# An encoder layer on one core: the transposes of an even chunk's linear attention output and their copy, set earlier in the second sweep

## The chip, the core and the metric

The kernel runs on one core of a Trainium2 chip. A core has a matrix engine (TensorE, PE in the profile, with its weight loads as PEld), a vector engine (VectorE, DVE), a scalar engine for activations and copies (ScalarE, ACT), a general one (GpSimd, POOL), and SyncE (SP), which here issues nearly all DMAs. Each engine works through its own instructions in their order and waits on semaphores for what it needs from others. The metric is the device time of one execution in microseconds (us), lower is better.

## What is computed

One layer of a hybrid encoder on a sequence of 2048 rows of width 1024, in float32. An input projection feeds two groups. Group A is a bidirectional gated linear attention with 4 heads, worked in chunks; group B is a latent attention with 4 heads, whose queries and keys come from compressed and normalised projections, with a rotary part. Both outputs go through one output projection, a residual and a layer norm.

```
h = x @ w_in
g_q, g_k, g_v, g_gate, g_lr_f, g_lr_b, m_cq, m_ckv, m_kr, m_gate = split(h)
o_a = rms_norm(gla(fwd) + gla(bwd)) * silu(g_gate)          # group A
o_b = softmax(q_nope k_nope' + q_rope k_rope') v * silu(m_gate)   # group B
out = layer_norm(alpha * x + concat(o_a, o_b) @ w_out)
```

What matters here is the piece of group A at the end: the sum of both directions is normalised per head, multiplied by the gate, and turned so that the features lie on the partitions, as the output projection needs it.

## The kernel before

Products are made in a split form: an operand is cut into a high and a low part, and three products (high by high, high by low, low by high) are added up. Suffixes `h` and `l` on names mean these parts.

The program has a first sweep over the 16 chunks of 128 rows (backward direction, group A), a second sweep over them in the other direction (`sweep_c`, line 1219), the attention of group B, and the output projection. The change touches the second sweep alone. It runs in 8 steps, numbered 0 to 7 here, of two chunks each, an even one and an odd one. A chunk needs, among others:

- `c_ip`: the products `ipm` of the chunk's rows with the weights of the compressed queries and keys; from them ScalarE and VectorE make `cq`, `ckv` and the rotary key `krs`
- `c_tm` (line 1438): four transposes `tm` of `cq` (two), `ckv` and `krs`; copies of them are `cqT`, `ckvT` and (`c_krT`) the key's rotary part. These are the "q's and kv's parts"
- `c_pqr` and `c_tq`: the rotary queries, turned in `tq`, and read by `c_qrTh` on ScalarE and `c_qrTl` (line 1490) on VectorE
- `c_Ob`: the products `Ob` of group A with the state; `c_og` then writes `og`, the normalised and gated output
- `c_ot` (line 1576): four transposes of `og` into the PSUM tile `ot`
- `c_oT` (line 1581): the copy of `ot` to the SBUF tile `oT` on ScalarE, scaled by the norm's weight
- `c_soT` (line 1585): the store of `oT` to DRAM, issued by SP
- `c_xh`, `c_xl`: the high part `xch` of the next rows on ScalarE and their low part `xcl` on GpSimd

A step also has the gate of group B for both chunks: the products `pz` in eight pieces of twelve (`c_pz`), three passes of ScalarE over `gm` and one of VectorE (`c_gm1` to `c_gm4`), and the products `pq` of the queries with their high and low part (`c_qah`, `c_qal`) and the stores of these.

The order of all this is written out by hand. Each part has a place: a number in units of a step, counted from the start of its own step, in the table `PLACE_C` (line 169), with a pair of numbers where the even and the odd chunk have one each. Step 0 takes its numbers from `PLACE_C_FIRST`, step 7 from `PLACE_C_LAST`. All parts of all steps are sorted by step plus place and issued in that order, and `in_order` (line 416) ties each engine to it, SP too:

```
p = PLACE_C[n]
p = (last and PLACE_C_LAST.get(n)) or (not st and PLACE_C_FIRST.get(n)) or p
todo.append((st + (p if j is None else p[j]), len(todo), fn, a))
...
for _, _, fn, a in sorted(todo, key=lambda e: e[:2]):
    with self.in_order(last):
        fn(*a)
```

So a place of 1.736 lies in the next step at 0.736, beside what that step has there.

Two pools matter. The PSUM pool `tr` (line 554) has two buffers, shared by `tm`, `pqr`, `tq` and `ot` of all chunks: a new tile takes a buffer when the last reader of the one before is through. The SBUF pool `w1` (line 1223) has one buffer for each name, unless a number is given; `oT` has one:

```
self.w1 = ctx.enter_context(self.tc.tile_pool(name="wk2", bufs=1, reuse_waits="tile"))
d["oT"] = self.w1.tile([P, H, P], F32, tag="oT", name=f"oT{d['c']}")
```

Some places of steps 1 to 6, before the change (even chunk, odd chunk): `tm` 0.532 and 1.152, `ot` 0.926 and 1.312, `oT` 0.998 and 1.347, `soT` 1.119 and 1.736, `qrTl` 1.25 and 1.687, `vh` 0.732 and 1.218, `krT` 0.848 and 1.233, `pqr` 0.849 and 1.355. The next step's `xch` for its even chunk stands at 0.81 of a step, the `gm` passes at 0.823 to 0.837. The pieces of `pz` stand at 0.25 to 0.559. The store of the odd chunk in step 0 stands at 1.538.

Of the kernel before, what the change touches and what calls it, by code (L numbers as in the profile page):

```python
# [174 lines left out]
    tm=(0.532, 1.152),  # L175
    pqr=(0.849, 1.355),
    tq=(1.06, 1.482),
    ot=(0.926, 1.312),
    xh=(-0.19, -0.054),
    qhb=(-0.048, 0.321),  # L180
    MMh=(-0.034, 0.412),
# [9 lines left out]
    ckvTh=(0.64, 1.277),  # L191
    krT=(0.848, 1.233),
    qrTh=(1.16, 1.587),
    oT=(0.998, 1.347),
    oib=(0.24, 0.881),
    oia=(0.235, 0.863),
    ss=(0.278, 1.005),
# [60 lines left out]
    ot=(1.009, 1.378),  # L258
# [15 lines left out]
    oT=(1.14, 1.433),  # L274
# [49 lines left out]
    ot=(0.915, 1.082),  # L324
# [15 lines left out]
    oT=(1.011, 1.153),  # L340
# [2092 lines left out]
```

## Time and profile before

| | |
|---|---|
| median of three runs | 1276.6 us (1276.45 to 1277.14) |
| the profiled execution | 1275.83 us |
| its span, first to last instruction | 1274.0 us |
| TensorE busy | 1253.9 us, 98% of the span |
| VectorE, ScalarE, GpSimd busy | 938.3, 875.2, 849.4 us |
| second sweep | from about 378 us to some 606 us |
| one of its steps | about 30 us |

The profile is of one execution. Busy time of TensorE is from the start of a product to its modelled end, and products overlap, so that a busy engine may still have a little room. A row of the timeline has the start, the duration, the engine, the line, the operation, the tiles (out<-in, without buffer numbers), the operand shapes and the count; in brackets stand the idle time of the engine before it and what ended that. A row of the list of waits has who waited, for whom, the total in us, how often, and the longest. A row of the table of stretches has the stretch, its length, then busy time and count of PE, PEld, DVE, ACT and POOL, the granted TensorE clock, the share of the DMA engines and what they moved in GB/s. A row of the DMA issues has the tiles, the queue, the count, the size of each and the median time from issue to landing.

### The profile page before, as it was taken

To read this page: it belongs to the slowest core of one execution; us is meant where nothing else is said; L and a number is where in the kernel's file an instruction comes from. 1 tells how busy PE (TensorE), PEld (TensorE's weight loads), DVE (VectorE), ACT (ScalarE), POOL (GpSimd) and SP (SyncE) were. 2 spreads that over 40 slices of the span, in tenths; PEclk is the share of its full clock that TensorE was granted. 3 is DMA by queue.
4 is the path that set the end of the run, shared out by engine and by line. 5 is a ranking of instruction groups with operands and counts; after the bars stand their busy time and mean duration, and the time that the engine had idled before them with its cause. 6 is when DMAs were issued, how large, how long until landed. Compare 5 with 4: busy or idle time off the path is not lost.

```text
span 1274.0 us, 20184 instructions
## 1 busy us (share of the span) xinstructions
PE 1253.9 (98%) x6928; PEld 1109.6 (87%) x6928; DVE 938.3 (74%) x1702; ACT 875.2 (69%) x1553; POOL 849.4 (67%) x550
## 2 busy tenths in 40 slices
PE   7999999999999999999999999999999999999997
PEld 7999999999989999999788888888888888788886
DVE  6866675656675455555798888888888888738897
ACT  7765656766675655665688888888888888624365
POOL 0144545363667666672188888889999999965774
PEclk9999999999999999999999999999999999999999
DMA  9332524353575565565601111121223111568962
GB/s 300 96 96 63 168 81 156 106 155 102 191 254 169 180 222 184 182 196 166 177 1 42 42 42 42 42 58 59 59 58 91 53 43 31 174 207 297 342 214 98
DMA packets 122518, 166.81 MB, mean 131 GB/s; under 512 B 18502, under 2 KB 71118, under 8 KB 121776
## 3 DMA queue, kind: packets, MB, share of 16 engines
q1 hardware_dynamic: 114256, 163.39, 40.2%
q0 software_dynamic: 768, 2.10, 0.5%
q8 instruction: 55, 0.90, 0.4%
q10 hardware_dynamic: 7392, 0.03, 0.3%
q14 instruction: 47, 0.39, 0.2%
HBM read 106.72 MB, written 58.75 MB: 130 GB/s over the span
## 4 chain that ended last, share of the span: by engine, by line
PE 88%; ACT 3%; POOL 2%; DVE 2%; DMA 2%; issue 1%; SPq 1%; DVEq 0%; POOLq 0%; ACTq 0%
PE o L454 4%; PE o L456 4%; PE pS L1649 4%; PE o L455 4%; PE pS L1651 4%; PE pS L1650 4%; PE pS L1652 4%; PE pS L1653 4%; PE ipa L454 4%; PE ipa L456 4%; PE ipa L455 4%; PE pz L455 2%; PE pz L456 2%; PE pz L454 2%; PE ipg L454 2%; PE ipg L455 2%
## 5 line engine op out<-in xcount | busy, mean ns | idle before, releaser
L406 POOL TENSOR_TENSOR pl<-s,ph 128x1024 fp32r<-128x1024 f32 x128 | 306.1, 2414 | 56.4 <-ACT ph L400 56.4
L1671 DVE TENSOR_TENSOR rm<-pS,rm 128x512 f32<-128x512 f32 x210 | 144.7, 689 | 26.3 <-ACT s L1658 20.7
L1695 DVE TENSOR_TENSOR s<-s,mb 128x1024 f32<-128x1024 f32 x128 | 151.1, 1212 | 9.4 <-PE mb L1689 9.3
L1658 ACT ACTIVATE s<-pS 128x1024 f32<-128x1024 f32 x128 | 131.2, 1025 | 37.6 <-PE pS L1653 33.2
L400 ACT ACTIVATE ph<-s 128x1024 fp32r<-128x1024 f32 x128 | 134.9, 1057 | 13.4 <-PE o L456 12.7
L1699 ACT ACTIVATE s<-s 128x1024 f32<-128x1024 f32 x128 | 131.4, 1051 | 13.4 <-DVE s L1695 13.3
L454 PE MATMUL ipa<-wah,xah 128*128 128x384 f32 (+1 forms) x384 | 130.2, 339 | 6.3 <-ACT wah L400 6.2
L1112 POOL TENSOR_TENSOR Us<-Us,cw 128x512 f32<-128x512 f32 x16 | 18.2, 1134 | 175.8 <-DVE Us L1110 167.7
L455 PE MATMUL ipa<-wal,xah 128*128 128x384 f32 (+1 forms) x384 | 125.2, 326 | 0.1
L456 PE MATMUL ipa<-wah,xal 128*128 128x384 f32 (+1 forms) x384 | 125.2, 326 | 0.0
L1649 PE MATMUL pS<-qh,ckvT_h 128*128 128x512 f32 x256 | 102.5, 401 | 0.8 <-DVE rm L1671 0.4
L454 PE MATMUL o<-ph,vh 128*128 128x512 f32 x256 | 101.1, 395 | 0.0
L1652 PE MATMUL pS<-rh,krs 128*128 128x512 f32 x256 | 99.8, 390 | 0.0
L1650 PE MATMUL pS<-ql,ckvT_h 128*128 128x512 f32 x256 | 99.8, 390 | 0.0
L456 PE MATMUL o<-ph,vl 128*128 128x512 f32 x256 | 99.8, 390 | 0.0
L1651 PE MATMUL pS<-qh,ckvT_l 128*128 128x512 f32 x256 | 99.8, 390 | 0.0
L1653 PE MATMUL pS<-rl,krs 128*128 128x512 f32 x256 | 99.8, 390 | 0.0
L455 PE MATMUL o<-pl,vh 128*128 128x512 f32 x256 | 99.8, 390 | 0.0
L1722 DVE TENSOR_TENSOR ap<-ap,s 128x512 f32<-128x512 f32 x120 | 83.1, 693 | 3.5 <-ACT ap L1714 0.7
L454 PEld LDWEIGHTS ipa<-wah,xah 128*128 128x128 f32 x384 | 73.4, 191 | 7.3 <-ACT wah L400 6.7
L454 PE MATMUL pz<-xch,wzh 128*128 128x256 f32 x256 | 74.8, 292 | 0.0
L455 PEld LDWEIGHTS ipa<-wal,xah 128*128 128x128 f32 x384 | 73.4, 191 | 1.3 <-DVE wal L406 0.7
(446 smaller groups left out, 3895.9 us busy)
## 6 DMA issues: line engine op xcount, KB each, us to landing
xcf<-xT_dram SPq DMA_DIRECT2D x16, 512.0 KB, 4.9
xr<-x_dram SPq DMA_DIRECT2D x16, 512.0 KB, 6.9
xaf<-xT_dram SPq DMA_DIRECT2D x14, 512.0 KB, 3.8
wb<-wO_dram SPq DMA_DIRECT2D x16, 256.0 KB, 3.0
oib<-oi_s SPq DMA_DIRECT2D x16, 256.0 KB, 3.8
qdb<-qd_s SPq DMA_DIRECT2D x16, 256.0 KB, 4.3
SU<-su_s SPq DMA_DIRECT2D x16, 256.0 KB, 4.6
ub<-u_s SPq DMA_DIRECT2D x16, 256.0 KB, 4.2
```

The source lines that it names most:

```text
L400: return nc.scalar.activation(dst, src, AF.Copy).ins
L406: return e.tensor_tensor(dst, src, hi.bitcast(F32), ALU.subtract).ins
L454: mm(out, ah, bh, start=start, stop=False)
L455: mm(out, ah, bl, start=False, stop=False)
L456: mm(out, al, bh, start=False, stop=stop)
L1649: mm(ps[:, e], kh, qh, start=True, stop=False)
L1650: mm(ps[:, e], kh, ql, start=False, stop=False)
L1651: mm(ps[:, e], kl, qh, start=False, stop=False)
L1652: mm(ps[:, e], kr, rh, start=False, stop=False)
L1653: mm(ps[:, e], kr, rl, start=False, stop=True)
L1671: V.tensor_tensor(d["rm"], src[:, e], d["rm"], ALU.max)
L1695: V.tensor_tensor(s, s, d["mb"][:, None, :].to_broadcast([P, 2, QB]), ALU.subtract)
```

## The change

In the table for steps 1 to 6 two numbers differ, both for the even chunk alone: the transposes `ot` are placed directly behind `tm` of the same chunk, and their copy `oT` behind the copies of `tm`'s parts. Nothing else is touched; the tables of step 0 and step 7 and the place of the store stay.

```
@@ PLACE_C
-    ot=(0.926, 1.312),
+    ot=(0.533, 1.312),
...
-    oT=(0.998, 1.347),
+    oT=(0.7, 1.347),
```

## The prediction

> **What bounds the kernel now.** I read the page first (TensorE busy nearly throughout), then a table of stretches over one step of the second sweep, then the list of who waited for whom, and at last the timeline of each engine in the step from about 421 to 451 us, which I call step 2 (the one whose even chunk is 4). The rows are times from the span's start.
>
> ```profile
> 451.00:481.00 30.00, 29.87 (x218) 28.78 (x217) 15.61 (x56) 17.87 (x47) 20.02 (x21) 1.00 0.58 194
> ...
> PEld pz L455 <- POOL xcl L406: 1.0, 5, 0.3
> ...
> PE Ob L1547 <- POOL qlb L406: 0.6, 1, 0.6
> ```
>
> The first row is one step of 30 us: TensorE is busy for 29.87 us of it, the other compute engines for 15 to 20. That looks like a TensorE bound with plenty of room elsewhere. The second row corrects it. Five times in steps 1 to 6, once per step, the first `pz` product that reads `xcl` had to wait for GpSimd, 1.0 us in total; the third shows the same kind of wait once, at an `Ob` product after step 6. So at one point of every step TensorE is already the one that waits, and the work that it waits for has no slack at all. I follow that work back from `xcl`.
>
> ```profile
> 442.57 1.06 ACT L400 ACTIVATE xch<-xcf 128x1024 fp32r<-128x1024 f32 x1 [2.12 <-PE pz L456]
> ...
> 446.92 1.23 DVE L1337 TENSOR_TENSOR gm<-pz,gm 128x1024 f32<-128x1024 f32 x1 [6.00 <-ACT gm L1334]
> ...
> 448.56 0.38 ACT L1396 ACTIVATE sqm<-ipm 128x256 f32<-128x256 f32 x1 [1.51 <-DVE rope L1598]
> ...
> 450.28 0.62 ACT L400 ACTIVATE qhb<-qdb 128x512 fp32r<-128x512 f32 x1
> ...
> 450.98 1.29 POOL L406 TENSOR_TENSOR qlb<-qdb,qhb 128x512 fp32r<-128x512 f32 x1 [0.97 <-ACT qhb L400]
> ...
> 453.75 2.40 POOL L406 TENSOR_TENSOR xcl<-xcf,xch 128x1024 fp32r<-128x1024 f32 x1
> ...
> 456.21 0.39 PE L455 MATMUL pz<-xcl,wzh 128*128 128x256 f32 x1
> ```
>
> The chain runs: the last `pz` product lets ScalarE overwrite `xch` (442.57); behind that copy stand the three passes over `gm`; VectorE ends the gate (446.92), and goes on to the rope of the key; ScalarE, which waited 1.51 us for that rope, squares `ipm` (448.56), copies the next `xch`, then `qhb` (450.28); GpSimd, which waited for `qhb`, does `qlb`, `MMb`, `krs` and at 453.75 `xcl`, which ends at 456.15; TensorE goes on at 456.21. Every link is either back to back with the one before or has its wait on the one before. **Whatever delays the `xch` copy at 442.57 by a time delays the next step by the same time**; TensorE's work beside it (`ipm`, `pqr`, `Ob`, `ipm`, `tq`, `Ob`, `tm`) is 0.2 us too short to be the later one.
>
> **The change part by part.** In steps 1 to 6 the four transposes `ot` of the even chunk go from behind `pqr` to directly behind `tm`, and the copy `oT` on ScalarE from behind the logarithm of `rm` to in front of `vh`. No instruction is added or removed, and no DMA: the store of `oT` keeps its place on SP. The data is long there (the even chunk's `og` is finished at place 0.391). What changes is what the moved instructions stand in front of, and whose buffers they take.
>
> *The transposes.*
>
> ```profile
> 429.12 0.60 PE L1579 MATMUL ot<-ident,og 128*128 128x128 f32 x4
> 429.48 0.36 PE L454 MATMUL pz<-xch,wzh 128*128 128x256 f32 x1
> ...
> 439.40 0.27 PE L1442 MATMUL tm<-ident,krs 128*128 128x128 f32 x1
> ...
> 438.38 0.41 DVE L406 TENSOR_TENSOR qrTl<-tq,qrTh 128x256 fp32r<-128x256 f32 x1
> ...
> 409.62 0.27 PE L1442 MATMUL tm<-ident,krs 128*128 128x128 f32 x1
> ...
> 410.73 0.41 DVE L406 TENSOR_TENSOR qrTl<-tq,qrTh 128x256 fp32r<-128x256 f32 x1
> ```
>
> Four of them take 429.48 - 429.12 = 0.36 us of TensorE, 0.09 each. At the old place they stood beside the chain, where TensorE has 0.2 us to spare; at the new one they stand ahead of the last `pz` products, whose end starts the chain. So 0.36 us per step is a loss and what leaves the old place is no gain (it only lengthens the wait for `xcl`). The pool `tr` has two PSUM buffers. At the new place one holds `tm`, the other the `tq` of the chunk before, which `qrTl` on VectorE reads last. In step 2 `qrTl` ends at 438.38 + 0.41 = 438.79, before `tm` is through at about 439.5: no wait, and steps 3 to 6 repeat this order. In step 1 it is otherwise: `qrTl` ends at 410.73 + 0.41 = 411.14, while TensorE arrives at 409.62 + 0.09 = 409.71. It waits 1.43 us there, with the rest of `pz` queued behind it. **Step 1 costs 1.43 + 0.36 = 1.79 us.**
>
> *The copy.* `oT` has one buffer, and the store of the odd chunk before (`soT`, place 1.736, that is 0.736 of this step) reads it. Before, the copy came at 0.998, long after that store. Now it comes at 0.70, ahead of it, so the copy has to wait until the store has landed, and `vh`, `xch`, the three `gm` passes and the key's copy `krs` are queued behind it on ScalarE. The store is queued on SP behind `qah` and `qal`, two stores of 512 KB each that only start when `pq` is done.
>
> ```profile
> 437.23 0.53 SPq L1365 DMA_DIRECT2D qh_s<-qah  x1
> 438.49 0.52 SPq L1365 DMA_DIRECT2D ql_s<-qal  x1
> ...
> 439.75 1.48 SPq L1586 DMA_DIRECT2D oa_s<-oT  x1
> ...
> 469.69 1.17 SPq L1586 DMA_DIRECT2D oa_s<-oT  x1
> ...
> 499.47 1.17 SPq L1586 DMA_DIRECT2D oa_s<-oT  x1
> ...
> 529.49 0.95 SPq L1586 DMA_DIRECT2D oa_s<-oT  x1
> ...
> 560.73 0.43 SPq L1586 DMA_DIRECT2D oa_s<-oT  x1
> ```
>
> ```profile
> oa_s<-oT SPq DMA_DIRECT2D x1, 256.0 KB, 5.1
> ...
> oa_s<-oT SPq DMA_DIRECT2D x1, 256.0 KB, 4.1
> ...
> oa_s<-oT SPq DMA_DIRECT2D x1, 256.0 KB, 5.3
> ...
> oa_s<-oT SPq DMA_DIRECT2D x16, 256.0 KB, 2.2
> ```
>
> The first three are the time from issue to landing of the store in steps 2, 4 and 6, the last the median of all sixteen. For steps 3 and 5 the profile gives none; I take 4.1, that of step 4, whose queue looks the same. Steps 2 to 6 have such a store in the way; in step 1 it is step 0's, which has an earlier place of its own (0.538) and is not.
>
> ```profile
> 429.84 0.67 ACT L1583 ACTIVATE oT<-ot,gn_c 128x512 f32<-128x512 f32 x1
> 430.42 0.19 ACT L467 ACTIVATE rm_l<-ssm 128x2 f32<-128x2 f32 x1
> ...
> 440.14 0.31 ACT L400 ACTIVATE vh<-ckv 128x128 fp32r<-128x128 f32 x1
> ...
> 472.51 1.06 ACT L400 ACTIVATE xch<-xcf 128x1024 fp32r<-128x1024 f32 x1 [2.12 <-PE pz L456]
> ...
> 502.29 1.06 ACT L400 ACTIVATE xch<-xcf 128x1024 fp32r<-128x1024 f32 x1 [2.12 <-PE pz L456]
> ...
> 532.07 1.06 ACT L400 ACTIVATE xch<-xcf 128x1024 fp32r<-128x1024 f32 x1 [2.12 <-PE pz L456]
> ...
> 561.84 1.06 ACT L400 ACTIVATE xch<-xcf 128x1024 fp32r<-128x1024 f32 x1 [2.12 <-PE pz L456]
> ```
>
> From the start of `oT` to that of the next instruction go 0.58 us; `vh` takes 0.31 less the same overlap of 0.09, 0.22. So `xch` can start 0.80 us after the landing. Without the wait the copy would be free: ScalarE idles for 2.12 us in front of each `xch`. With it, against the old starts:
>
> - step 2: 439.75 + 5.1 + 0.80 - 442.57 = 3.08
> - step 3: 469.69 + 4.1 + 0.80 - 472.51 = 2.08
> - step 4: 499.47 + 4.1 + 0.80 - 502.29 = 2.08
> - step 5: 529.49 + 4.1 + 0.80 - 532.07 = 2.32
> - step 6: 560.73 + 5.3 + 0.80 - 561.84 = 4.99
>
> Each is above the 0.36 of the transposes and contains it, since `xch` waits for the later of the two. They add up because the store hangs on `pq` of its own step and so moves along with what was lost before. Behind step 6 it is the wait of `Ob` for `qlb` that passes the delay on. Together 14.55, with step 1 **16.3 us**. Against the profiled execution, 1275.83 (span 1274.0 and 1.83 around it), that is 1292.1; the median of the runs lies 0.8 above that execution, so I forecast 1276.6 + 16.3 = **1292.9 us**.
>
> Nothing is to be had at the old places: ScalarE's copy stood behind `qhb` and `krs`, the last instructions there on which the chain hangs.
>
> [...]
>
> **The rivals.**
> - *The copy does not have to wait for the store* (it lands in memory that the store doesn't read). Then 1.43 + 6 x 0.36 = 3.6 us stay: 1280.2. One buffer of that name in the pool speaks against it. If TensorE's wait in step 1 and the chain also have more give than I read, it is within 0.2%.
> - *The store lands as fast as the median, 2.2.* Steps 2 to 4 then cost 0.36 each, step 5 529.49 + 3.0 - 532.07 = 0.42, step 6 1.89; with step 1 5.2, so 1281.8. The three landings measured speak against it.
> - *Faster.* The copy leaves its old place, where it takes 0.58 us of ScalarE in each of six steps. If the chain to `xcl` ran through ScalarE behind that place, 3.5 us would go: 1273.1. It decides where an instruction that GpSimd needs before `xcl` is placed later than 0.998. I find none; `krs`, at 0.972, is the last.
> - *Part of the loss is hidden*, for instance half of step 6 because the last step has other waits: 16.3 - 2.5. Or the two landings that I took as 4.1 are 5.3: + 2.4.
>
> **How the numbers follow.** The forecast has a chance of 0.77, with its own range of 1287 to 1298: landings shorter by a microsecond in each of five steps below, the unknown landings and a longer wait in step 6 above. No wait for the store 0.06, the store fast 0.04, both slower by over 0.2% (2.6 us, about what a measurement of this kernel can tell from no change); within 0.2% 0.08; faster 0.05. For 8 in 10 the range reaches down to the first two: 1279 to 1298. Faster 0.05, same 0.08, slower 0.87.
>
> **What would show it.** Right, if in steps 2 to 6 `oT` of the even chunk starts on ScalarE after an idle time that ends with the landing of the odd chunk's store, `xch` starts 2 to 5 us later in its step, and TensorE idles that much in front of `Ob` and the `pz` product that reads `xcl`; in step 1 TensorE waits about 1.4 us for `qrTl`. The stretch of one step grows from 29.9 to about 32. Wrong, if `oT` starts in the idle time before `xch` without a wait, if the waits on TensorE do not follow those on ScalarE, or if the stores land sooner.

## Result and profile after

| | before | after |
|---|---|---|
| median | 1276.53 us (1276.25 to 1277.14, 4 runs) | 1296.62 us (1295.98 to 1297.23, 4 runs) |
| the profiled execution | 1275.83 | 1297.23 |
| its span | 1274.0 | 1295.4 |

The changed kernel is slower by 20.1 us; the ratio is 1.0157, with an interval of 1.0145 to 1.017. The forecast was 1292.9, slower by 16.3. The direction and the mechanism were those of the forecast, the size was 3.8 us short.

First the page of the changed kernel (span, then busy time of each engine), and after it the row of one step of the second sweep in the table of stretches; its columns are those of the row shown in the prediction.

```profile
span 1295.4 us, 20175 instructions
...
PE 1259.3 (97%) x6928; PEld 1111.9 (86%) x6928; DVE 940.4 (73%) x1702; ACT 874.9 (68%) x1553; POOL 849.0 (66%) x550
```

```profile
453.00:486.00 33.00, 30.25 (x210) 28.83 (x209) 15.69 (x57) 17.46 (x47) 19.77 (x20) 0.95 0.54 176
```

The work is the same, the span is 21.4 us longer. A step takes 32 to 33 us where it took 30; ScalarE and GpSimd do in it what they did before, and TensorE, which had been busy for 29.87 of 30 us, is now busy for 30.25 of 33. The clock of 0.95 in this row was 1.00 before; the prediction says nothing of it, and it comes back below.

Who waited for whom, first on ScalarE (400 to 600 us), then on TensorE (400 to 630 us): engine, line, what it waited for, then the total in us, how often, and the longest.

```profile
ACT oT L1583 <- DMA oa_s<-oT: 22.9, 5, 6.3
```

```profile
PE Ob L1546 <- POOL MMb L406: 8.4, 5, 2.9
PE pz L454 <- DVE og L1573: 2.1, 4, 0.7
PE ot L1579 <- DVE qrTl L406: 1.4, 1, 1.4
PE ipm L456 <- POOL xcl L406: 1.0, 1, 1.0
PE Ob L1547 <- POOL qlb L406: 0.9, 1, 0.9
PE pqr L454 <- ACT oT L1583: 0.8, 1, 0.8
```

The copy `oT` waits five times for the landing of the store that reads the same buffer, once in each of steps 2 to 6. Not all of the 22.9 us is loss: ScalarE had been idle there for 2.12 us a step in front of `xch`. TensorE's own wait is above all the 8.4 us in front of `Ob`, again five times. Two rows were foreseen (`Ob`, and `ot` for `qrTl`), the last one, `pqr`, was not. Nor was the row of `pz` for `og`, but it adds nothing by itself: at the same four places the weight load of the next product, which reads `xcl`, still waits 0.16 to 0.41 us for GpSimd, so `xcl` is the later one there.

The timeline of ScalarE around these copies:

```profile
448.01 0.69 ACT L1583 ACTIVATE oT<-ot,gn_c 128x512 f32<-128x512 f32 x1 [5.06 <-DMA oa_s<-oT]
448.60 0.30 ACT L400 ACTIVATE vh<-ckv 128x128 fp32r<-128x128 f32 x1
448.80 1.05 ACT L400 ACTIVATE xch<-xcf 128x1024 fp32r<-128x1024 f32 x1
...
480.91 0.69 ACT L1583 ACTIVATE oT<-ot,gn_c 128x512 f32<-128x512 f32 x1 [3.56 <-DMA oa_s<-oT]
...
512.86 0.69 ACT L1583 ACTIVATE oT<-ot,gn_c 128x512 f32<-128x512 f32 x1 [3.74 <-DMA oa_s<-oT]
...
545.26 0.69 ACT L1583 ACTIVATE oT<-ot,gn_c 128x512 f32<-128x512 f32 x1 [4.22 <-DMA oa_s<-oT]
...
579.75 0.69 ACT L1583 ACTIVATE oT<-ot,gn_c 128x512 f32<-128x512 f32 x1 [6.29 <-DMA oa_s<-oT]
```

SP's queue and TensorE at the two places that the prediction named:

```profile
441.18 0.52 SPq L1365 DMA_DIRECT2D ql_s<-qal  x1
442.44 1.17 SPq L1586 DMA_DIRECT2D oa_s<-oT  x1
```

```profile
411.93 0.63 PE L1579 MATMUL ot<-ident,og 128*128 128x128 f32 x4 [1.39 <-DVE qrTl L406]
```

The store of the odd chunk is issued at 442.44, behind `ql_s`; the copy starts at 448.01, 5.57 us later, and `xch` 0.79 behind it with no idle time of its own (0.80 had been reckoned). Where the profile has the landing of this store (steps 2, 4 and 6: 447.93, 512.77 and 579.67), the copy starts 0.08 to 0.09 us after it. In step 1 the transposes wait 1.39 us for `qrTl` (1.43 reckoned).

### The profile page after: what moved, and what is told of

The parts are those of the page before. It is cut to its first block, busy times and chain, and to the rows that moved or that the text cites. A ratio compares the mean times of both kernels' runs of the same rounds, so it can differ in the third digit from the quotient of the medians.

```text
span 1295.4 us, 20175 instructions
## 1 busy us (share of the span) xinstructions
PE 1259.3 (97%) x6928; PEld 1111.9 (86%) x6928; DVE 940.4 (73%) x1702; ACT 874.9 (68%) x1553; POOL 849.0 (66%) x550
## 4 chain that ended last, share of the span: by engine, by line
PE 55%; ACT 4%; DVE 3%; DMA 3%; issue 1%; POOL 1%; SPq 1%; DVEq 0%; ACTq 0%
PE o L454 4%; PE o L456 4%; PE o L455 4%; PE pS L1649 4%; PE pS L1650 4%; PE pS L1651 4%; PE pS L1653 4%; PE pS L1652 4%; PE pw L455 2%; PE pw L456 2%; PE pw L454 2%; DMA oa_s<-oT 1%; PE pz L455 1%; PE pz L454 1%; PE pz L456 1%
```

## Experiments

Nine kernels were run. Two measures of the traces are used beside the times. A **step's shift** is the start of the first `pz` product that reads `xcl` in the next step, less the same start in before's trace, less what was already lost one step earlier. And for the store's part, a step is cut in two: from the first `pq` product to the copy `oT` (the store's way), and from `oT` to the first `pq` product of the next step (the chain).

### The transposes alone

```
-    oT=(0.7, 1.347),
+    oT=(0.998, 1.347),
```

The changed kernel with the copy back at its old place.

> The copy keeps its old place, only the transposes are early. If the copy's wait for the odd chunk's store carries the loss, 1.43 us for qrTl in step 1 and 6 x 0.36 us of transposes ahead of the gate products remain, 3.6 us: about 1280, and no half-clock stretch. If the early transposes themselves (their PSUM buffer, their place) carry it, the time stays near 1293 to 1297.

Measured: 1280.95 (1280.81 to 1281.84) against 1275.8 of before, measured beside it, ratio 1.004, interval 1.0025 to 1.0055. The five waits of `oT` for the store are gone. So about 5 us of the 20 are the transposes', and about 15 the copy's. The shifts of steps 1 to 6 are 2.04, 0.35, 0.46, 0.42, 0.43 and 1.50: the 0.36 of the prediction is confirmed in steps 2 to 5, step 1 has 0.25 more than its 1.79, and step 6 has 1.1 more than expected.

### The store ahead of its neighbours

```
-    soT=(1.119, 1.736),
+    soT=(1.119, 1.45),
```

The change in full, but the odd chunk's store stands earlier in SP's queue, ahead of the two large stores.

> Both are early, and the odd chunk's store goes from 1.736 to 1.45, ahead of the stores of q, so that it has landed when the copy comes. Store theory: the five waits of oT on a DMA are gone, 3.6 us remain: about 1280. Rival (the copy in front of vh and xch costs by itself, or the turn-over of PSUM does): 1290 or more.

Measured: 1282.21 (1280.37 to 1282.83), ratio 1.005, interval 1.0033 to 1.0067. The list of ScalarE's waits has no `oT` that waits for a DMA any more, and the shifts are those of x1 (2.00, 0.40, 0.43, 0.43, 0.42, 1.50). These are of the profiled execution, which took 1280.37; the other three took 1.5 to 2.5 us more, and there is no trace of them. The interval overlaps that of x1.

### Two buffers

```
-        self.gkv_b = w1.tile([P, H, P], F32, tag="oT", name="gkv_b")[:, 0]
+        self.gkv_b = w1.tile([P, H, P], F32, tag="oT", name="gkv_b", bufs=2)[:, 0]
...
-        d["oT"] = self.w1.tile([P, H, P], F32, tag="oT", name=f"oT{d['c']}")
+        d["oT"] = self.w1.tile([P, H, P], F32, tag="oT", name=f"oT{d['c']}", bufs=2)
```

The change in full, with a second buffer for the copy (an earlier tile shares its name and so has to be given two as well).

> Both are early, oT has two buffers, the store keeps its place: the wait is taken away in another way. Store theory: about 1280, as in the run with the earlier store. If that run is fast and this one is not, it is the traffic of the store and not the wait for the buffer.

Measured: 1281.04 (1280.99 to 1281.86), ratio 1.0041, interval 1.0026 to 1.0056, again without a wait of `oT` for the store. Store first and second buffer are two independent ways to take the same wait away, and both end where the transposes alone end. The one buffer under a store that has not landed is the cause of the 15 us, together with what follows from that wait (see the low clock below); the early copy as such costs nothing that these runs can tell.

### Step 6 alone

```
                 p = (last and PLACE_C_LAST.get(n)) or (not st and PLACE_C_FIRST.get(n)) or p
+                if st in (6,):
+                    p = dict(ot=(0.533, 1.312), oT=(0.7, 1.347)).get(n, p)
```

The kernel before, with the new places in step 6 only.

> Both are early in step 6 alone, whose store lands last. The store theory gives 5.0 us, 1281.5; with one stretch of 3.4 us at half clock behind the wait, as the changed kernel's trace has it there, 1.7 more: 1283.2. If only the transposes' 0.36 us count per step, 1276.9.

Measured: 1284.65 (1283.88 to 1286.79), ratio 1.007, interval 1.0055 to 1.0085. One step in the changed form costs 8.85 us, more than either expectation, and its shift is 7.86, where the sum had 4.99. The part that the sum describes is right:

```profile
566.83 1.05 ACT L400 ACTIVATE xch<-xcf 128x1024 fp32r<-128x1024 f32 x1
```

This is 4.99 behind the old 561.84, of which 0.17 was there before the step. The other 3 us are two things that the sum does not have. The first is the 1.1 us of x1. The second is in the table of stretches (stretch, length, busy time and count of PE, PEld, DVE, ACT and POOL, granted clock, DMA share, GB/s):

```profile
572.62:576.03 3.41, 0.42 (x2) 0.18 (x1) 2.07 (x7) 3.35 (x9) 3.03 (x4) 1.00 0.10 10
576.03:579.44 3.41, 2.54 (x10) 2.45 (x11) 2.12 (x8) 2.04 (x8) 3.41 (x3) 0.50 0.92 328
579.44:582.86 3.42, 3.42 (x11) 3.03 (x10) 2.35 (x9) 0.60 (x2) 3.18 (x4) 0.50 0.36 128
```

Behind a stretch in which TensorE was busy for only 0.42 of 3.41 us, the granted clock is 0.50 for two such stretches. In the changed kernel's own stretch of this kind, from 591.15 to 594.56, an `ipm` product starts every 0.37 us (592.58, 592.95, 593.32), and behind it every 0.20 (594.71, 594.90, 595.10). In x4's second stretch TensorE is busy for the whole 3.42 us. From the copy to the next `pq` this execution takes 24.35 us; x9 below, with the same step and no slow stretch, takes 22.37. So the clock is 2.0 of the 3 us.

### Where the 1.1 us of step 6 come from

TensorE in step 6, first before, then in x1 (chunk 13 is the odd one of this step):

```profile
580.01 0.60 PE L1579 MATMUL ot<-ident,og 128*128 128x128 f32 x4
580.36 0.36 PE L454 MATMUL pqr<-wqr_h,cqT_h 128*128 128x256 f32 x1
```

```profile
583.86 0.60 PE L1579 MATMUL ot<-ident,og 128*128 128x128 f32 x4
585.24 0.39 PE L454 MATMUL pqr<-wqr_h,cqT_h 128*128 128x256 f32 x1 [0.78 <-ACT oT L1583]
```

`pqr` had come directly behind `ot`, 0.35 after its start; now it comes 1.38 after it, because it waits for the copy of the odd chunk's `ot`. The only thing that `pqr` and this copy share is the pool `tr`, so the wait is read as `pqr` of chunk 13 having got the buffer of `ot`. The profile leaves buffer numbers out, so this is inferred and not seen. It is not a matter of strict turns: the places put the tiles of `tr` in the same order in both kernels from `tq` of chunk 12 on, and with two buffers handed out in turn, `pqr` directly behind `ot` would get the other one in both. How the pool came to choose otherwise, and in step 6 alone, stays open. The next kernel is x1 with this `pqr` ahead of that `ot`, so that it can't get that tile's buffer:

```
                 p = (last and PLACE_C_LAST.get(n)) or (not st and PLACE_C_FIRST.get(n)) or p
+                if st == 6 and n == "pqr":
+                    p = (0.849, 1.305)
```

> The change with the copy oT of the even chunk back at 0.998 (as in x1), and in step 6 alone the rotary queries pqr of the odd chunk 13 placed ahead of ot of that chunk, so that pqr takes the PSUM buffer of an older tile and has no copy oT to wait for. Theory: the 1.50 us that step 6 still cost in x1 are 0.4 for the transposes ahead of the last pz and 1.1 for pqr of chunk 13, which had come into the buffer of ot and waited for its copy; here the 1.1 go, so 1281.0 - 1.1 = 1279.9, and pqr of chunk 13 starts without a wait for oT. Rival: the 1.1 come from somewhere else in step 6 (the transposes at their new place); then the time stays at 1281.0, and step 6 still costs 1.5.

Measured: 1280.67 (1280.12 to 1281.97), ratio 1.0035, interval 1.0022 to 1.0047. By the times alone this can't be told from x1's 1.004 (1.0025 to 1.0055). The trace tells it: the wait is not in the list any more, and step 6's shift is 0.41 where it was 1.50. So `pqr` standing behind `ot` costs the 1.1 us. The profiled execution gave 0.9 of this back near its end, in the output projection, 0.5 of it at a wait of TensorE for a copy by ScalarE that x1's execution does not have.

### The transposes behind `pz`

```
-    ot=(0.926, 1.312),
+    ot=(0.702, 1.312),
```

The kernel before, with the transposes moved only as far as the stretch behind the last `pz` product.

> Before, with the transposes ot of the even chunk moved earlier too, but only to 0.702, behind the last pz product (0.559) and among the ipm products; the copy oT stays at 0.998. Theory: the 0.36 us of the four transposes count only ahead of the end of pz, and the wait for qrTl in step 1 is over by then; steps 1 to 5 then cost 0.0 to 0.1 each. Only pqr of chunk 13, which comes into the buffer of ot of that chunk here too, costs 1.1 in step 6: 1276.5 + 1.1 = 1277.6. Rival: TensorE is the bound everywhere, or any earlier place costs because ot takes a buffer of the pool sooner: 0.4 a step again, and with step 6 1279 to 1280.

Measured: 1277.95 (1276.71 to 1280.37, 11 runs) against 1276.29 (15 runs), ratio 1.0015, interval 1.0006 to 1.0024. The shifts of steps 1 to 5 are 0.07, 0.04, 0.07, 0.08 and 0.07, that of step 6 is 1.39, with the same wait of `pqr`:

```profile
581.22 0.38 PE L454 MATMUL pqr<-wqr_h,cqT_h 128*128 128x256 f32 x1 [0.78 <-ACT oT L1583]
```

Four transposes of 0.36 us cost 0.4 a step ahead of the end of `pz`, and next to nothing behind it. They and the wait for `qrTl` cost where they stand, not because they are early. With step 6 the profiled execution loses 1.7 us in these steps.

### The copy behind the gate

```
-    oT=(0.7, 1.347),
+    oT=(0.84, 1.347),
```

The change with the same single buffer and the store where it was, but the copy behind `xch` and the `gm` passes in ScalarE's queue (the copy `krs` of the key's part stands behind `oT` here and in the changed kernel).

> The change with the copy oT of the even chunk at 0.84 in place of 0.70: still ahead of the old place and still behind the same single buffer and the store of the odd chunk, but behind xch and the three gm passes in ScalarE's queue. Theory: the wait for the store costs because xch and the gm passes are queued behind it; with these in front the store has landed by the time the copy is reached, and the time is that of x1, 1281.0 (up to 1282 if the copy waits a little and holds krs or sqm up). Rival: the single buffer itself is what costs, wherever the copy stands ahead of the store's landing; then most of the 15 us stay, and the time is above 1290.

Measured: 1281.43 (1281.25 to 1282.45), ratio 1.004, interval 1.0028 to 1.0053: the time of x1. ScalarE's timeline in step 2:

```profile
444.80 1.06 ACT L400 ACTIVATE xch<-xcf 128x1024 fp32r<-128x1024 f32 x1 [2.56 <-PE pz L456]
...
448.97 0.67 ACT L1583 ACTIVATE oT<-ot,gn_c 128x512 f32<-128x512 f32 x1
449.54 0.27 ACT L400 ACTIVATE krs<-tm 128x128 fp32r<-128x128 f32 x1
450.74 0.38 ACT L1396 ACTIVATE sqm<-ipm 128x256 f32<-128x256 f32 x1 [0.94 <-PE pqr L456]
```

The store was issued at 441.54 and landed 5.5 us later, at 447.0: behind the start of `xch`, but ahead of the copy. When the queue reaches the copy there is nothing left to wait for. Its 0.57 us fall into the idle time that ScalarE has in front of `sqm`.

### The low clock

The changed kernel's stretches of 3.41 us, taken so that they begin and end with the changes of the clock:

```profile
553.60:557.02 3.42, 1.99 (x11) 1.56 (x10) 1.83 (x10) 2.46 (x10) 2.72 (x3) 1.00 0.44 139
458.03:461.44 3.41, 1.59 (x12) 1.35 (x12) 3.02 (x15) 2.42 (x13) 3.41 (x4) 1.00 0.86 267
461.44:464.86 3.42, 3.21 (x13) 2.96 (x14) 3.13 (x12) 1.56 (x7) 3.42 (x5) 0.50 0.22 62
587.74:591.15 3.41, 0.89 (x5) 0.72 (x6) 1.86 (x8) 2.69 (x9) 3.12 (x3) 1.00 0.53 130
591.15:594.56 3.41, 3.41 (x13) 3.11 (x12) 2.66 (x10) 1.92 (x5) 3.41 (x4) 0.50 0.95 316
```

Half clock follows the two stretches in which TensorE was busy for 1.59 and 0.89 of 3.41 us (a share of 0.47 and 0.26); it does not follow the one with 1.99 (0.58). Between its first 13 and its last 6 us, before has no stretch at half clock, nor has any of x1, x2 and x3 (mean clock of these four executions 0.998 to 0.999, of the changed kernel's 0.996). To test this without touching the waits, TensorE was given something to do in two of them:

```
         d["Ob"], d["Ob1"], d["rp"] = t[:, :, 0], t[:, :, 1], t[:, 0, 1]
+        if d["c"] in (6, 14):
+            for _ in range(20):
+                self.nc.tensor.transpose(t[:, 0, 0], self.ident, self.ident)
```

> The change with 20 transposes of the identity added ahead of the first Ob product of chunks 6 and 14 (steps 3 and 7), written into the tile that these products then overwrite; 0.09 us each, 1.8 us, less than the 2.3 and 2.9 us that TensorE waits there for MMb. Theory: the two stretches of 3.4 us at half clock come because TensorE was busy for less than about half of the 3.4 us before; filled to 0.8 and more, both go, and with them 2 x 1.7 = 3.4 us: 1296.6 - 3.4 = 1293.2, although work was added. Rival 1: only one of them goes: 1294.9. Rival 2: the low clock has nothing to do with how busy TensorE was, or the time lost there was hidden behind other waits: 1296.6 to 1297.

Measured: 1298.75 (1296.57 to 1300.12), ratio 1.0173, interval 1.0159 to 1.0187. The time missed all three expectations, and the trace of the profiled execution (1296.57) shows why. First the two filled places, at the same times as in the changed kernel (the changes of this execution's own clock lie elsewhere, as the second list shows):

```profile
458.03:461.44 3.41, 2.71 (x20) 2.07 (x19) 3.13 (x17) 2.75 (x12) 3.41 (x4) 1.00 0.72 214
461.44:464.86 3.42, 3.42 (x31) 3.42 (x31) 3.07 (x12) 1.89 (x6) 3.34 (x5) 1.00 0.51 138
587.74:591.15 3.41, 1.81 (x15) 1.40 (x13) 1.93 (x5) 2.99 (x9) 3.11 (x4) 1.00 0.32 58
591.15:594.56 3.41, 3.33 (x19) 3.12 (x20) 2.85 (x13) 2.15 (x6) 3.41 (x5) 1.00 0.95 285
```

```profile
490.92:494.33 3.41, 1.59 (x12) 1.35 (x12) 3.10 (x15) 2.42 (x13) 3.41 (x4) 1.00 0.92 274
494.33:497.74 3.41, 3.28 (x14) 3.04 (x15) 3.12 (x11) 1.55 (x6) 3.41 (x5) 0.50 0.25 58
```

Both filled places keep the full clock. But the gap of the next step, left empty, fell into one stretch with again 1.59 us of work, and the clock dropped there. Within the changed kernel's execution the two drops, at 461.44 and 591.15, are 38.0 stretches of 3.41 us apart. Where the stretches lie against the program differs between executions: from 461.44 there to 494.33 here are 9.64 of them. (The other three runs, of which there is no trace, have a mean clock of 0.994, lower than the 0.995 to 0.996 of the changed kernel; presumably more than one gap was hit in them.) So all five gaps were filled:

```
+        for _ in range({6: 14, 8: 10, 10: 6, 12: 6, 14: 16}.get(d["c"], 0)):
+            self.nc.tensor.transpose(t[:, 0, 0], self.ident, self.ident)
```

> As x8_keep_tensore_busy, but with transposes of the identity ahead of the first Ob product of all five even chunks whose Ob has to wait for MMb: 14, 10, 6, 6 and 16 of them for chunks 6, 8, 10, 12 and 14, at some 0.12 us each (1.7, 1.2, 0.7, 0.7 and 1.9 us, each shorter than the wait there). Theory: half clock follows a stretch of the clock's own 3.41 us grid in which TensorE was busy for less than about half; x8 filled two of the five gaps and one of the others then fell into such a stretch. With all five filled no stretch is left, in any execution: clock 0.998 in all runs, and 1296.6 - 3.4 = 1293.2, up to 1294.5 where the filling runs a little over. Rival: the half clock is hidden, that is, what it costs TensorE is time that it would wait for the store anyway; then the stretches go and the time stays at 1296 to 1297.

Measured: 1293.76 (1293.04 to 1295.16), ratio 1.0144, interval 1.0127 to 1.016. No stretch at half clock is left between the first 13 and the last 6 us of the profiled execution, and the mean clock of the four runs is 0.997 to 0.999. The interval overlaps that of the changed kernel (1.0145 to 1.017), so the gain itself is read from the traces. TensorE and ScalarE in steps 2 and 3 (in this order: first `pq` product, copy, first `pq` product of the next step), of the changed kernel, of x8 and of x9:

```profile
448.01 0.69 ACT L1583 ACTIVATE oT<-ot,gn_c 128x512 f32<-128x512 f32 x1 [5.06 <-DMA oa_s<-oT]
470.24 0.28 PE L454 MATMUL pq<-cqT_h,wabs_h 128*128 128x256 f32 x1
480.91 0.69 ACT L1583 ACTIVATE oT<-ot,gn_c 128x512 f32<-128x512 f32 x1 [3.56 <-DMA oa_s<-oT]
502.00 0.28 PE L454 MATMUL pq<-cqT_h,wabs_h 128*128 128x256 f32 x1
```

```profile
468.05 0.28 PE L454 MATMUL pq<-cqT_h,wabs_h 128*128 128x256 f32 x1
480.82 0.69 ACT L1586 ACTIVATE oT<-ot,gn_c 128x512 f32<-128x512 f32 x1 [5.66 <-DMA oa_s<-oT]
503.05 0.28 PE L454 MATMUL pq<-cqT_h,wabs_h 128*128 128x256 f32 x1
```

```profile
446.35 0.69 ACT L1585 ACTIVATE oT<-ot,gn_c 128x512 f32<-128x512 f32 x1 [4.65 <-DMA oa_s<-oT]
467.44 0.28 PE L454 MATMUL pq<-cqT_h,wabs_h 128*128 128x256 f32 x1
478.31 0.69 ACT L1585 ACTIVATE oT<-ot,gn_c 128x512 f32<-128x512 f32 x1 [3.76 <-DMA oa_s<-oT]
499.41 0.28 PE L454 MATMUL pq<-cqT_h,wabs_h 128*128 128x256 f32 x1
```

From the copy to the next `pq` the chain takes 470.24 - 448.01 = 22.23 us with a half-clock stretch in it (changed kernel, behind step 2), and 503.05 - 480.82 = 22.23 in x8 behind step 3; without one it takes 21.09 (502.00 - 480.91), 21.09 (467.44 - 446.35) and 21.10 (499.41 - 478.31). All five steps, read in the same way:

| | step 2 | 3 | 4 | 5 | 6 |
|---|---|---|---|---|---|
| first `pq` to `oT`: the forecast's landings | 11.70 | 10.70 | 10.71 | 10.95 | 13.62 |
| changed kernel | 12.17 | 10.67 | 10.86 | 11.32 | 13.39 |
| x8 | 12.12 | 12.77 | 10.79 | 10.90 | 13.47 |
| x9 | 11.77 | 10.87 | 10.78 | 10.85 | 12.52 |
| `oT` to the next first `pq`: changed kernel | **22.23** | 21.09 | 21.08 | 21.10 | **23.20** |
| x8 | 21.09 | **22.23** | 21.08 | 21.08 | 22.34 |
| x9 | 21.09 | 21.10 | 21.07 | 21.10 | 22.37 |

(The last column of the lower rows is longer because step 7 has places of its own, and because it holds the 1.1 us of `pqr`.) The bold ones are the chains with a half-clock stretch. It costs 22.23 - 21.09 = 1.14 and 23.20 - 22.37 = 0.83, together **2.0 us** of the 3.4 that one would get from two stretches at half speed. Part of each falls where TensorE waits at full clock too: at the `pz` products with which the first stretch begins, step 4 of the changed kernel has waits for `og` and `xcl` (0.46 and 0.21 us), and behind the second one x9 waits 0.46 us for `MMb` at the odd chunk's `Ob`, where the changed kernel does not wait. So the 3.4 us of the expectation were too many, and that x9 came out near 1293.2 is in part luck: its five ways from `pq` to the copy add up to 56.8 us, 1.6 less than in the changed kernel. The upper rows show this other thing that moves between executions: in step 3 the way to the landing of the same store took 10.67, 12.77 and 10.87.

## Why the prediction was right, and where it was short

- **Which work bounds, and that a delay of `xch` passes on whole: right.** x4 moved `xch` by 4.82 us net in one step and lost that, beside the two terms that the sum lacked. x7 moved nothing but the copy's place in the queue and lost none of the store's part.
- **The copy has to wait for the odd chunk's store: right,** shown by x2 and x3, which take the wait away in two ways and leave 1282.2 and 1281.0. The rival that the copy needs no wait, and that of a fast store, gave 1280.2 and 1281.8; x3 and x2, in which the copy has no store to wait for, took 1281.0 and 1282.2.
- **The landings: right in size.** In the table the forecast's five sum up to 57.7 us and the changed kernel's to 58.4. Two of them were not in the profile and were taken from a neighbour; they came out within 0.4 us. That is luck in part, since in step 3 the same way took 2.1 us more in x8. From issue to copy the changed kernel shows 5.57 us in step 2, against the 2.2 us from issue to landing of the median store before, which the second rival took.
- **The transposes: right** at 0.36 a step (0.33 to 0.46 measured in x1 to x3), and for step 1, where 1.79 was reckoned and 2.0 measured. x6 shows that they cost by standing ahead of the end of `pz`.
- **The first step that failed: "whose buffers they take".** The prediction followed the buffers of `tr` for the even chunk's transposes in step 1 and wrote that steps 3 to 6 repeat step 2. It put the cost for tiles that come later at nothing. In step 6 `pqr` of the odd chunk waited for the copy of `ot`: 1.1 us (x1, x5, x6). That this is the buffer of `ot` is inferred from the wait.
- **The second: TensorE's clock was taken as constant.** "TensorE idles that much in front of `Ob`" was foreseen, and that the clock falls to 0.50 behind some of that idle time was not: 2.0 us in the profiled execution (x8, x9, table). The sign itself came only in part: in front of the `pz` product that reads `xcl` TensorE idles for 0.6 us in all, and 2.1 us went to the product ahead of it.
- **The whole of the profiled pair.** Of the 21.4 us between the two profiled executions, the terms above give 16.3 + 0.2 (step 1) + 0.7 (landings) + 1.1 + 2.0, less 0.5, since from the copy onwards a step was 0.05 to 0.23 quicker than reckoned. This is 19.8, and the shifts of the table below add up to 19.9. Another 1.5 us lie ahead of step 1 (0.65) and from step 7 on (0.82), where the kernels do the same, and are taken as spread between executions: x8 and x9, which also do the same up to step 1, come there 0.3 and 0.6 ahead of before. The medians differ by 20.1.
- **That the time fell into the range is luck in part.** The range reached up to 1298 for the two unknown landings and a longer wait in step 6; what filled it was above all the clock and `pqr`.

| step | 1 | 2 | 3 | 4 | 5 | 6 |
|---|---|---|---|---|---|---|
| forecast | 1.79 | 3.08 | 2.08 | 2.08 | 2.32 | 4.99 |
| shift, changed kernel | 2.02 | 3.30 | 3.16 | 2.16 | 2.63 | 6.64 |
| shift, x9 | 2.01 | 2.92 | 2.20 | 2.07 | 2.16 | 4.94 |

Without slow stretches (x9) each step comes within 0.22 us of the forecast. In step 6 that is chance: the way to the copy was 1.1 us shorter than forecast (12.52 for 13.62), and the wait of `pqr` took the 1.1 back.

No version was found that beats the kernel before: taking away the store's wait leaves the 5 us of the transposes, and taking these behind `pz` leaves the 1.1 us of `pqr` or a little more.

## What to carry to other kernels

Before an instruction is moved earlier, ask which buffer it writes and whether that buffer's last reader is a DMA: then its price is the landing of that DMA (here 3.56 to 6.29 us of idle time a step), and everything queued behind it on the same engine pays it. In a pool with two buffers, look at the waits of the later tiles too, up to the end of the loop: here a tile that the change did not touch came to wait for a slower reader (0.78 us). And when a change leaves TensorE idle, look at its granted clock behind that: here it was 0.50 for one or two stretches of 3.41 us behind idle times of 2.26 to 2.9 us.

## What the hardware did that was not expected

- **The clock fell behind idle times of 2.26 to 2.9 us.** The stretches at half clock are 3.41 us long, or two of these, and follow a stretch of 3.41 us in which TensorE was busy for 0.42, 0.89 or 1.59 us; behind the one with 1.99 it stayed at 1.00. In step 3 of the changed kernel the longest single idle time in front of the drop was 2.27 us, as this row of TensorE's timeline shows. Whether the share of busy time counts or the length of one gap is not settled by these traces: ahead of each drop stood a gap of 2.26 to 2.9 us, and the longest in the second sweep without a drop was 1.43.

```profile
459.58 0.39 PE L1546 MATMUL Ob<-MMb,qhb 128*128 128x256 f32 x1 [2.27 <-POOL MMb L406]
```

- **At half clock, being busy for most of a stretch did not restore it.** In x4 a stretch with 2.54 of 3.41 us busy was followed by another one at half clock; those with 3.21, 3.28, 3.41 and 3.42 were followed by full clock.
- **Added work probably made the kernel faster.** x9 runs 52 more transposes than the changed kernel, and its median is 2.9 us lower (1.7 by the two ratios, with intervals that overlap, so the times alone do not prove it). x8, with 40 more and gaps left open, came out 2.1 higher, also with an interval that overlaps.
- **The same store lands at different times.** In step 3 the way from `pq` to the copy was 10.67, 12.77 and 10.87 us in three executions in which SP issues the same DMAs in the same order; nearly all of the difference lies behind the issue (4.07, 6.16 and 4.27 us from there to the copy). Why is not known.
